# Late input projections cut into pieces of two k steps and spread over rounds 1 to 21

## The chip, the cores and the metric

The kernel runs on one core of a Trainium2 chip. The metric is the device time of one execution in microseconds (us), the smaller the better. Engines are named as in the profile: PE (TensorE, matmuls), PEld (its weight loads), DVE (VectorE), ACT (ScalarE), POOL (GpSimd), SP (SyncE, which here only issues transfers).

## The reference, cut to what matters

One layer of a decoder trunk on 1024 positions of width 1024, float32. The change lies in the first of its three parts:

```python
z = rmsnorm(h, norm_mix_g) @ w_in                 # 3840 columns: 30 blocks of 128
a_q, a_f, a_i, a_g, b_q, b_k, b_v, c_in = split(z)
o_a = hgrn2_mix(a_q, a_f, a_i, a_g, ...)          # 4 heads, a gated linear recurrence
o_b = dilated_window_mix(b_q, b_k, b_v)           # 4 heads of 64: windowed softmax attention
o_c = rwkv7_mix(c_in, ...)                        # RWKV-7
h = h + concat(o_a, o_b, o_c) @ w_out             # 8 blocks of 128 on each side
h = h + conv_glu_ffn(rmsnorm(h), ...)
h = h + sigmoid(rmsnorm(h) @ ple_gate) * (p @ ple_proj)
return rmsnorm(h)
```

## The kernel before

**Products of float32.** Every big product is made of three passes in a rounded format: `split2` and `split_x` divide an operand into a high part (a cast on ACT) and a low part (a subtraction on DVE or POOL), and `mm3` (L137, L139, L141) multiplies high by high, low by high and high by low into one PSUM bank. A weight block of 128 columns has 8 k steps; one k step on 512 positions is three matmuls, one block on one half of the positions 24.

**Stages.** First come the norm and RWKV-7, with 18 of the 22 remaining input blocks projected between its steps (`project_rest`); then HGRN and attention together, which is where the change lies (about 400 to 590 us in the profile); then the output projection (`phase_out`), the feed-forward part and the gated embedding.

**The order in HGRN and attention.** `interleave` walks a written list of letters, and each letter takes one step of a generator. A runs HGRN heads 0 and 2 one behind the other, B heads 1 and 3 from round 6 on, C attention (two groups of two heads, in the 22 rounds of `TURNS`), M what is left of `project_rest`, and F `project_late`: the last four input blocks, `self.rest` = 29, 18, 22, 23 (the values of the second attention group, the values of heads 2 and 3, the output gate of head 3). There are 36 rounds of C, A, B, F. F takes a step in rounds 1, 3, 6, 9, 12, 15, 18, 20 and 21 (`LATE`).

**What a step of F is.** One step is one half of the positions of one block: the weight load (for the first half), 24 matmuls into one PSUM tile `zp`, the `finish` (a product with the row scale, L425, or for the gate block also a sigmoid and another product, L320, L428, L430), and the store of the half to memory. After the eighth step, the ninth allocates `self.O`, the split operands of the output projection, in the memory of the split input `self.X`, and splits all finished blocks in `self.done`: 6 and 7 (RWKV), 0 and 1 (HGRN heads), 4 (attention). Each `o_split` is two casts on ACT (L160) and one subtraction each on DVE and POOL (L162). Blocks that finish later are split when they finish.

**Buffers.** `zp` comes from the PSUM pool `mx` of four banks, which HGRN and attention use for all their small results: `hsc` (scores of a level of the recurrence, L925 and L951), `hkv`, `hpo`, `vt` (transposes), `swt`, `swo`, `swd` (attention, L1130, L1143, L204). The attention scores `swq` (L1104) and the output projection `dp` have a pool of their own.

**Who orders the queues.** The framework places instructions on the engines' queues at compile time: an instruction's place in the program is its priority, a model of time says what is ready, and the queues then run in order on the chip.

Of the kernel before, what the change touches and what calls it, by code (L numbers as in the profile page):

```python
# [21 lines left out]
ND = 8  # L22
# [43 lines left out]
def interleave(order, streams):  # L66

    live = dict(streams)
    while live:
        for s in order:  # L70
            if s in live and next(live[s], STOP) is STOP:
                del live[s]


def handover(a, b, steps=14):

    for _ in range(steps):
        next(a)
        yield
    for i, _ in enumerate(b):  # L80
        if i == 1:
            for _ in a:
                yield
        yield
# [5 lines left out]
class Trunk:  # L90
# [231 lines left out]
    def phase_mix(self):  # L322
        nc, tc = self.nc, self.tc
        self.mix_norm()
        with tc.tile_pool(name="slots", bufs=1) as slots:
            self.slots, self.NSLOT = slots, 8
            self.rwkv()
        self.O, self.done = None, []
        for p in (0, 1):
            self.o_split(6 + p)  # L330
        with tc.tile_pool(name="hg", bufs=1) as slots, tc.tile_pool(name="sw", bufs=1) as sp:
            self.slots, self.NSLOT = slots, 11
            self.hgrn_setup()
            self.sp = sp
            self.swmask = sp.tile([P, T], F32, name="swmask")
            nc.scalar.dma_start(self.swmask, self.a["swm"])
            A = handover(self.hgrn_head(0), self.hgrn_head(2))
            B = handover(self.hgrn_head(1), self.hgrn_head(3))
            order = ["C", "A"] + ["M"] * 24
            for r in range(36):  # L340
                order += "C" * (r in self.TURNS) + "A" + "B" * (r > 5) + "F" * (r in self.LATE)
            interleave(order, {"A": A, "B": B, "C": self.swa(sp), "F": self.project_late(self.rest), "M": self.more})

    LATE = (1, 3, 6, 9, 12, 15, 18, 20, 21)

    TURNS = [i * 33 // 22 for i in range(1, 23)]

# [84 lines left out]
    def project_late(self, js):  # L432


        nc = self.nc
        for j in js:
            w = self.load_w(self.a["w_in"][j])
            t = self.keep.tile([P, T], F32, tag="zst", name=self.nm("zst"), bufs=2)
            d = self.zpool.tile([P, T], F32, tag=f"z{j}", name=f"z{j}")
            kind = (j - 8) % 4 if j < 24 else 2  # L440
            turn = j < 24 and kind < 3
            for hf in (0, 1):
                ps = self.mxp.tile([P, HT], F32, tag="mx", name=self.nm("zp"))
                self.dense({hf: ps}, w, self.X, ND, halves=(hf,))
                dst = slice((hf ^ turn) * HT, ((hf ^ turn) + 1) * HT)
                r = self.R[:, hf * HT:(hf + 1) * HT]
                self.finish(kind, t[:, dst], *((ps[:, ::-1], r[:, ::-1]) if turn and hf else (ps, r)))
                nc.sync.dma_start(d[:, dst], t[:, dst])
                if hf:
                    self.z[j] = d  # L450
                yield
        self.O = self.xall()
        for k in self.done:
            self.o_split(k)

    def zload(self, j, pool_slot, eng=None):
        t = pool_slot("zl")
        (eng or self.nc.sync).dma_start(t, self.z[j])
        return t
# [1315 lines left out]
```

## Time and profile before

| | |
|---|---|
| runs, us | 1438.21, 1439.37, 1434.61 (median 1438.21) |
| the profiled execution, us | 1434.87, of which the span of its instructions is 1433.1 |
| mean granted clock of TensorE | 0.992 |
| busy share of the span | PE 97%, PEld 78%, DVE 74%, ACT 42%, POOL 27% |
| matmuls of `zp` | 192, from 402.2 to 521.2 us of the span |
| last late store | 526.6 us |

A busy PE is not a PE at its peak: matmuls overlap, and a stretch counts as busy though its clock is half of the full one.

### The profile page before, as it was taken

To read this page: it belongs to the slowest core of one execution; us is meant where nothing else is said; L and a number is where in the kernel's file an instruction comes from. 1 tells how busy PE (TensorE), PEld (TensorE's weight loads), DVE (VectorE), ACT (ScalarE), POOL (GpSimd) and SP (SyncE) were. 2 spreads that over 40 slices of the span, in tenths; PEclk is the share of its full clock that TensorE was granted. 3 is DMA by queue.
4 is the path that set the end of the run, shared out by engine and by line. 5 is a ranking of instruction groups with operands and counts; after the bars stand their busy time and mean duration, and the time that the engine had idled before them with its cause. 6 is when DMAs were issued, how large, how long until landed. Compare 5 with 4: busy or idle time off the path is not lost.

```text
span 1433.1 us, 22327 instructions
## 1 busy us (share of the span) xinstructions
PE 1383.1 (97%) x8638; PEld 1119.6 (78%) x8638; DVE 1054.6 (74%) x1635; ACT 604.1 (42%) x1015; POOL 380.9 (27%) x281
## 2 busy tenths in 40 slices
PE   6999999999999989999999999999999999999996
PEld 5778777777777867787788888888888888888885
DVE  6487353864657767458888888988898799777675
ACT  6511323123145465244544444334344444455542
POOL 2321012201122231121245445445453000002332
PEclk9999999999999989999999999999999999999998
DMA  6124112240442211652323232333324973441343
GB/s 219 45 81 118 61 35 80 71 119 31 150 145 104 85 50 46 234 200 100 143 79 105 96 110 98 109 110 110 102 98 136 340 244 105 123 147 45 133 156 116
DMA packets 79674, 167.61 MB, mean 117 GB/s; under 512 B 19920, under 2 KB 22224, under 8 KB 79568
## 3 DMA queue, kind: packets, MB, share of 16 engines
q1 hardware_dynamic: 66176, 146.39, 30.4%
q10 hardware_dynamic: 12368, 15.99, 3.3%
q0 software_dynamic: 1024, 3.80, 0.7%
q8 instruction: 68, 1.11, 0.3%
q14 instruction: 38, 0.31, 0.1%
HBM read 119.76 MB, written 46.40 MB: 116 GB/s over the span
## 4 chain that ended last, share of the span: by engine, by line
PE 50%; issue 2%; DVE 1%; POOL 1%; ACT 0%; DMA 0%; POOLq 0%; ACTq 0%; DVEq 0%
PE bg L1262 16%; PE bv L1262 12%; PE bv L1556 7%; PE bg L1556 7%; PE bv L137 1%; PE bv L139 1%; PE bv L141 1%; PE bg L137 1%; PE bg L141 1%; PE bg L139 1%; PE dp L141 1%; PE dp L139 1%; PE dp L137 1%; POOL wlo L116 0%; DVE h L1288 0%
## 5 line engine op out<-in xcount | busy, mean ns | idle before, releaser
L137 PE MATMUL dp<-xh,whi 128*128 128x512 f32 x544 | 189.1, 406 | 9.8 <-ACT xh L380 9.6
L139 PE MATMUL dp<-xl,whi 128*128 128x512 f32 x544 | 183.6, 395 | 0.7 <-DVE xl L381 0.6
L141 PE MATMUL dp<-xh,wlo 128*128 128x512 f32 x544 | 181.9, 393 | 0.3 <-POOL wlo L116 0.3
L116 POOL TENSOR_TENSOR wlo<-wraw,whi 128x512 fp32r<-128x512 f32 x60 | 81.1, 1353 | 309.0 <-ACT whi L114 278.9
L116 POOL TENSOR_TENSOR wlo<-raw,whi 128x512 fp32r<-128x512 f32 x84 | 134.7, 1622 | 76.1 <-ACT whi L114 76.1
L114 ACT CAST whi<-wraw 128x512 fp32r<-128x512 f32 x120 | 73.0, 617 | 179.9 <-PE dp L139 140.6
L1262 PE MATMUL bg<-t,whi 128*128 128x512 f32 x352 | 133.2, 389 | 0.0
L137 PEld LDWEIGHTS dp<-xh,whi 128*128 128x128 f32 x544 | 99.7, 189 | 34.3 <-ACT xh L380 9.6
L139 PEld LDWEIGHTS dp<-xl,whi 128*128 128x128 f32 x544 | 102.0, 188 | 25.1 <-DVE xl L381 2.4
L141 PEld LDWEIGHTS dp<-xh,wlo 128*128 128x128 f32 x544 | 102.4, 189 | 23.1 <-POOL wlo L116 0.8
L116 POOL TENSOR_TENSOR wlo<-s,whi 128x512 fp32r<-128x512 f32 x44 | 64.2, 1459 | 173.2 <-ACT whi L114 173.2
L1556 PE MATMUL bg<-t,whi 128*128 128x512 f32 x308 | 95.2, 390 | 0.0
L1556 PE MATMUL bv<-t,whi 128*128 128x512 f32 x308 | 94.8, 389 | 0.0
L114 ACT CAST whi<-raw 128x512 fp32r<-128x512 f32 x88 | 52.6, 619 | 94.6 <-issue 48.6
L114 ACT CAST whi<-s 128x512 fp32r<-128x512 f32 x66 | 38.9, 620 | 121.1 <-PE bg L1262 113.3
L1262 PEld LDWEIGHTS bg<-t,whi 128*128 128x128 f32 x352 | 66.1, 188 | 13.7
L190 POOL TENSOR_TENSOR rst<-rst,mhalf 128x4 f32<-128x4 f32 (+1 forms) x9 | 10.9, 1214 | 242.7 <-DVE rst L186 225.5
L116 DVE TENSOR_TENSOR wlo<-wraw,whi 128x512 fp32r<-128x512 f32 x60 | 46.6, 777 | 34.5 <-ACT whi L114 27.6
L1556 PEld LDWEIGHTS bv<-t,whi 128*128 128x128 f32 x308 | 57.8, 188 | 12.0
L1262 PE MATMUL bg<-t,wlo 128*128 128x512 f32 x176 | 67.2, 389 | 0.0
L1556 PEld LDWEIGHTS bg<-t,whi 128*128 128x128 f32 x308 | 57.8, 188 | 11.9
L1552 ACT CAST t<-t 128x512 fp32r<-128x512 f32 x77 | 47.8, 622 | 40.5 <-PE bv L1556 27.8
(415 smaller groups left out, 3396.1 us busy)
## 6 DMA issues: line engine op xcount, KB each, us to landing
raw<-in_ffn_up_dram SPq DMA_DIRECT2D x44, 512.0 KB, 3.5
wraw<-in_w_in_dram SPq DMA_DIRECT2D x30, 512.0 KB, 3.5
z<-zst SPq DMA_DIRECT2D x18, 512.0 KB, 3.4
gb<-ct SPq DMA_DIRECT2D x33, 256.0 KB, 2.1
t<-gb SPq DMA_DIRECT2D x33, 256.0 KB, 2.7
t<-gt SPq DMA_DIRECT2D x33, 256.0 KB, 2.7
zl<-z SPq DMA_DIRECT2D x16, 512.0 KB, 4.2
wraw<-in_ple_gate_dram SPq DMA_DIRECT2D x16, 512.0 KB, 3.4
```

The costliest lines, as they stand in the source:

```text
L114: self.cast = nc.scalar.copy(hi, src).ins
L116: eng.tensor_tensor(lo, src, hi.bitcast(F32), ALU.subtract)
L137: nc.tensor.matmul(ps[hf], wh, xh[hf], start=first, stop=False)
L139: nc.tensor.matmul(ps[hf], wh, xl[hf], start=False, stop=False)
L141: nc.tensor.matmul(ps[hf], wl, xh[hf], start=False, stop=last)
L190: nc.gpsimd.tensor_tensor(r2, r, self.mhalf[:, :n], ALU.pow)
L1262: nc.tensor.matmul(ps, w[part == 2][:, s], X[k][part == 1], start=start and k == part == 0, stop=k == 3 and part == 2, skip_group_check=no ...
L1552: nc.scalar.copy(xh, x)
L1556: nc.tensor.matmul(ps[m], wt[part == 2][:, m * P:(m + 1) * P], (xh, xl)[part == 1], start=k == part == 0, stop=k == NK - 1 and part == 2)
```

## The change

A step of F becomes two k steps (6 matmuls) of one half; every fourth step also finishes and stores the half, so that there are 32 steps in place of 8. A function `late(r)` in place of the list spreads them over rounds 1 to 21: ten rounds take one step and eleven take two. With two, one stands ahead of B and one behind it. `self.O` is allocated in round 22 in place of round 21, and the five splits are taken one a round, in rounds 22 to 26.

```diff
             for r in range(36):
-                order += "C" * (r in self.TURNS) + "A" + "B" * (r > 5) + "F" * (r in self.LATE)
+                n = self.late(r + 1) - self.late(r)
+                order += "C" * (r in self.TURNS) + "A" + "F" * (n // 2) + "B" * (r > 5) + "F" * (n - n // 2)
...
-    LATE = (1, 3, 6, 9, 12, 15, 18, 20, 21)
+    def late(self, r):
+        return min(32, max(0, r - 1) * 32 // 21) + max(0, min(6, r - 22))
...
                 ps = self.mxp.tile([P, HT], F32, tag="mx", name=self.nm("zp"))
-                self.dense({hf: ps}, w, self.X, ND, halves=(hf,))
+                for k in range(ND):
+                    self.mm3({hf: ps}, w(k), self.X[k], k == 0, k == ND - 1, (hf,))
+                    if k in (1, 3, 5):
+                        yield
...
         self.O = self.xall()
         for k in self.done:
             self.o_split(k)
+            yield
```

## The prediction

> **What bounds the kernel now.** I read the busy time of the engines by stretches first, because the page's 97% for PE says nothing of one stage. PE, PEld, DVE, ACT and POOL follow each stretch with the count of their instructions, then the granted clock, the share of the transfer engines and GB/s.
>
> ```profile
> 400.00:420.00 20.00, 19.93 (x174) 14.61 (x174) 11.38 (x28) 10.78 (x27) 7.87 (x7) 1.00 0.38 120
> 460.00:480.00 20.00, 20.00 (x266) 17.35 (x265) 16.16 (x32) 8.00 (x18) 5.46 (x6) 1.00 0.32 118
> 480.00:500.00 20.00, 20.00 (x175) 17.03 (x174) 14.60 (x38) 12.72 (x30) 4.76 (x4) 1.00 0.25 80
> 500.00:520.00 20.00, 17.05 (x83) 11.42 (x83) 13.27 (x24) 9.94 (x17) 4.04 (x3) 0.74 0.20 71
> 520.00:540.00 20.00, 18.24 (x195) 13.91 (x194) 15.34 (x34) 17.85 (x36) 9.36 (x9) 1.00 0.14 49
> 540.00:560.00 20.00, 18.48 (x197) 14.91 (x196) 15.94 (x34) 11.82 (x21) 4.16 (x3) 1.00 0.15 54
> 580.00:600.00 20.00, 18.15 (x83) 14.32 (x82) 8.78 (x12) 1.67 (x4) 2.92 (x2) 1.00 0.64 249
> ```
>
> Up to 500 us PE has no hole: whatever the order of the late projections is there, PE is the bound and reordering can't gain. From 500 to 520 PE is idle for 3 us and its clock is 0.74. That is a half clock for (1 - 0.74) x 20 / 0.5 = 10.4 us. From 520 on there are small holes. So I took the timeline of PE, then of DVE and ACT, around 500 us (start, length, engine, line, operation, count, and in brackets the idle time ahead and what ended it).
>
> ```profile
> 502.99 0.39 PE L141 MATMUL zp<-xh,wlo 128*128 128x512 f32 x1
> 505.94 1.34 PE L1104 MATMUL swq<-zl,zl 64*128 64x512 f32 x4
> 510.23 1.12 PE L951 MATMUL hsc<-qt,ks 128*64 128x64 f32 x16 [2.95 <-DVE qt L964]
> 512.01 2.50 PE L1104 MATMUL swq<-zl,zl 64*128 64x512 f32 x4
> 514.44 0.79 PE L139 MATMUL zp<-xl,whi 128*128 128x512 f32 x1
> 518.87 0.47 PE L141 MATMUL zp<-xh,wlo 128*128 128x512 f32 x1
> 519.18 0.39 PE L137 MATMUL zp<-xh,whi 128*128 128x512 f32 x1
> 519.41 0.39 PE L139 MATMUL zp<-xl,whi 128*128 128x512 f32 x1
> ...
> 499.45 0.69 DVE L162 TENSOR_TENSOR xl<-zl,xh 128x512 fp32r<-128x512 f32 x1 [2.25 <-ACT xh L160]
> 503.59 1.23 DVE L1033 TENSOR_TENSOR ho<-ho,hrs 128x1024 f32<-128x1024 f32 x1 [1.75 <-POOL hrs L1031]
> 509.40 0.68 DVE L964 TENSOR_TENSOR qt<-qt,hT 128x512 f32<-128x512 f32 x1
> 519.76 0.69 DVE L116 TENSOR_TENSOR wlo<-wraw,whi 128x512 fp32r<-128x512 f32 x1 [4.58 <-ACT whi L114]
> ...
> 501.37 0.62 ACT L160 CAST xh<-ob 128x512 fp32r<-128x512 f32 x1 [0.99 <-PE zp L141]
> 515.69 0.62 ACT L160 CAST xh<-zl 128x512 fp32r<-128x512 f32 x1 [3.64 <-PE zp L141]
> 519.11 0.62 ACT L114 CAST whi<-wraw 128x512 fp32r<-128x512 f32 x1 [2.80 <-PE zp L139]
> ```
>
> The reader sees a seesaw. While PE does the 24 matmuls of round 18 (497.7 to 503), DVE runs dry; its work then comes in one burst from 503.59 to 515 without a gap, the next level of the recurrence gets its `qt` only at 509.40, and PE stands for 2.95 us. The clock falls to half. In round 20 the same again: DVE stands for 4.58 us behind the lump, and ACT, whose queue is in order, stands for 3.64 and 2.80 us, since the split casts wait until the lump has left `self.X`. The bill of that comes behind 520.
>
> ```profile
> 524.08 0.69 PE L1104 MATMUL swq<-zl,zl 64*128 64x512 f32 x1 [0.60 <-DVE sden L1114]
> 531.62 1.15 PE L925 MATMUL hsc<-zl,hk 128*64 128x64 f32 x32 [1.16 <-ACT ob L1144]
> 559.47 1.06 PE L1039 MATMUL vt<-cst,ho 128*128 128x128 f32 x8 [1.18 <-DVE ho L1033]
> 584.73 1.06 PE L1039 MATMUL vt<-cst,ho 128*128 128x128 f32 x8 [1.79 <-DVE ho L1033]
> ```
>
> The last two follow a chain inside one head (square, sum, power on POOL, scaling, transpose), which the change does not touch.
>
> **What the change can give back.** Same matmuls, same casts, same transfers; only places change. (1) The hole of 2.95 us. (2) The half clock while PE works. Between 514.44 and 518.87 eleven matmuls start; at the full rate, 0.23 from 519.18 to 519.41, their ten intervals and one would take 2.3 us in place of 4.4, so 2.1 lost. From 510.23 to 514.44 lie 16 small matmuls, one of `zp` and four of `swq`, 4.2 us; half of that, 2.1, is lost if all of it is clock-bound. Together 4.2. (3) The holes of 0.60 and 1.16, which follow the clogged ACT queue. Sum 2.95 + 4.2 + 1.76 = 8.9 us. I take all of it, for with six matmuls at a time (6 x 0.23 = 1.4 us) neither DVE nor ACT is starved for longer than a level's own latency. The lower end is nothing (a hole of this kind opens elsewhere, see the rivals), the upper 8.9 plus the holes of 1.18 and 1.79, 11.9.
>
> **What it costs: more changes of work on PE.** Up to 24 more stretches of `zp`. The ends of the first lump show the price:
>
> ```profile
> 402.23 0.50 PE L137 MATMUL zp<-xh,whi 128*128 128x512 f32 x1
> 402.56 0.39 PE L139 MATMUL zp<-xl,whi 128*128 128x512 f32 x1
> 402.80 0.40 PE L141 MATMUL zp<-xh,wlo 128*128 128x512 f32 x1
> 407.59 0.39 PE L141 MATMUL zp<-xh,wlo 128*128 128x512 f32 x1
> 407.91 0.88 PE L951 MATMUL hsc<-qt,ks 128*64 128x64 f32 x16
> ```
>
> The first matmul holds the next back by 0.33 in place of 0.23, the last by 0.32: 0.2 us for each stretch, taking the change into it as no dearer than the one between two small kinds that it replaces. 24 x 0.2 = 4.8 at most; nothing at least, where the queue puts pieces side by side. Of 24 I take 18: rounds with two pieces (eleven of them) have only a level of B in between, and some will meet. 18 x 0.2 = 3.6 us, all on the path, as PE has no hole before 500.
>
> **What it costs: PSUM.** A `zp` bank is now held for four pieces. The pieces are 32 in 21 rounds, so four take 2.6 rounds; rounds 1 to 20 last some 6 us each (the first row below: 402.2 to 521.2), so a bank is held for 16 us, one behind the other, and the small results have three banks in place of four. They are held briefly:
>
> ```profile
> L137 PE MATMUL zp<-xh,whi x64: 387/389/796, 402.2 to 521.2; 128*128 128x512 f32 x64
> 526.31 0.69 PE L951 MATMUL hsc<-qt,ks 128*64 128x64 f32 x16
> 527.04 0.45 DVE L953 COPY_PREDICATED hS<-cmask,hsc 128x256 f32<-128x256 uint8 x1 [0.49 <-PE hsc L951]
> PE hsc L925 <- ACT ob L1144: 1.2, 1, 1.2
> ```
>
> A typical score tile is free again 1.2 us after its first matmul. The last row (from the waits of PE alone, 400 to 532 us) is its one wait of over 1 us for a bank: the scores need nothing that ACT's copy of `swo` makes but its bank. So with three banks I take one more such wait, 1.2 us; the lower bound is zero, the upper one such wait in every second of the 21 rounds, 12 us.
>
> **What moves and costs nothing.** Each half's finish, one store and, per block, one load on SP, two casts and the POOL and DVE subtractions move with it; counts are unchanged. The weight tiles turn over in the same order, but their release is spread, so ACT's waits of the 2.80 kind shrink; if they don't, they cost what they cost now. The results come in time: piece 8 falls in round 6 and attention reads block 29 in round 12; pieces 16 and 24 fall in rounds 11 and 16, read in rounds 22 and 29; block 23 ends in round 21 and is read in round 33. SP passes nothing that waits on them: only loads of `w_out` and of head inputs stand behind a store, and these have rounds to spare. The five splits, 10 casts of 0.62 on ACT with 5 subtractions each on DVE and POOL, now rank behind rounds 22 to 26. That takes them from ahead of attention's copies; the first reader is the output projection, whose first matmul starts near 552, so a round or two of delay has cover. If the projection came first, it would wait at most one split, 0.62 + 1.28 us (a cast and POOL's subtraction).
>
> **Sum.** -8.9 + 3.6 + 1.2 = -4.1 us against the profiled execution's 1434.87: 1430.8, so 1431. From about 590 us on PE is the bound almost to the end, so what is won early arrives. The profiled execution is a quick one: the runs were 1434.61 to 1439.37 with median 1438.21. What made two of them 3 to 5 us longer no trace shows; a second half-clock stretch would be of that size (4.2), and then the change could take that too. I add nothing for it. About 0.3%, 4.3 us, is what a measurement here can tell from no change.
>
> [...] The half clock began behind a hole of 2.95 us and, by the 0.74, lasted 10.4 us. [...]
>
> **Rivals.**
> - *The hole only moves.* DVE is 14 to 16 of 20 us busy in this stretch, and some burst may still meet a PE without filler. For it: rounds 18 to 21 used to bring 48 late matmuls and now bring 42, in small pieces that run out. Against: one piece is then always near. Then 7.2 us return: 1430.8 + 7.2 = 1438, within the bound.
> - *Three PSUM banks don't do* (slower). PE queues in order, so one small result without a bank holds everything behind it, and neighbours such as transposes (`vt`, four a head) and two to four `swt` a round want several banks at once. Each such wait is 1.16 us by the row at 531.62. It decides from nine on: -8.9 + 3.6 + 9 x 1.16 = +5.1. With twelve, 1443.5. Against: 1.2 us of holding. [...]
> - *Pieces meet and later holes close too.* No price for switches, and some of 1.18 and 1.79: 1434.9 - 8.9 - 1.5 = 1424.5.
> - *Nothing happens,* because the planner puts the pieces back together into lumps: 1434.9.
>
> **Chances.** Forecast 0.50 (its own range 1426 to 1435, by the switches at 0 to 4.8 and the bank waits at 0 to 4); the hole moves 0.17; PSUM 0.16; meet and close 0.12; nothing 0.05. The range reaches from just below the fourth case to between the hole's and the PSUM case: 1423 to 1441. Measured against a median that may stand above the profiled time, some two thirds of the forecast is faster by over 0.3%, with the fourth case 0.46; the rest of it, most of the moved hole and nothing give 0.34 the same; PSUM and a bad moved hole 0.20 slower.
>
> **What would show it.** Right: in PE's timeline pieces of 6 of `zp` from about 402 to 515; no half clock near 510; ACT's waits on `zp` under 1 us; casts of the splits spread behind 515; `dp` starting some 4 to 9 us earlier than 552. Wrong: PE holes before 500 that ACT or DVE copies of another tile end (banks), or the clock at half in another stretch, or stretches of 24 `zp` as before.

## The result, and the profile after

The changed kernel took 1442.73 us (median; 1438.74 to 1446.60), the kernel before 1438.28 (1434.61 to 1442.54): ratio 1.003, 95% interval 1.0021 to 1.0039. It is slower by some 4.4 us where 1431 was forecast. The profiled execution has a span of 1439.2 us.

The stretches of the stage in the changed kernel, with the columns of those shown of before:

```profile
400.00:420.00 20.00, 20.00 (x176) 14.55 (x174) 12.59 (x30) 10.97 (x27) 8.05 (x7) 1.00 0.42 144
460.00:480.00 20.00, 17.61 (x153) 13.38 (x152) 13.98 (x25) 7.65 (x14) 6.60 (x6) 0.91 0.39 139
500.00:520.00 20.00, 18.72 (x146) 13.20 (x144) 14.34 (x34) 12.17 (x30) 4.72 (x3) 1.00 0.33 108
520.00:540.00 20.00, 15.61 (x175) 11.73 (x175) 19.94 (x29) 15.84 (x30) 11.99 (x9) 1.00 0.16 56
540.00:560.00 20.00, 17.61 (x165) 12.83 (x165) 15.81 (x39) 12.45 (x25) 2.26 (x2) 1.00 0.22 74
```

The hole and the long half clock near 510 are gone (PE's clock is 1.00 there). But PE is idle for 4.4 us from 520 to 540, where DVE is busy for all of the 20 us with 29 instructions; before it had 34 in 15.3. DVE is not given more to do: its instructions are longer. The waits of PE from 400 to 590 us of the changed kernel (engine, line and tile waiting, what ended it, total us, times, longest):

```profile
PE hsc L957 <- DVE pT L1137: 2.4, 1, 2.4
PE hsc L931 <- DVE zst L432: 2.2, 1, 2.2
PE vt L1045 <- DVE hS L959: 1.7, 1, 1.7
PE vt L1045 <- DVE ho L1039: 1.6, 1, 1.6
PE swt L1136 <- ACT ob L1150: 1.4, 1, 1.4
PE swt L1136 <- DVE hS L959: 1.2, 1, 1.2
PE swt L1136 <- DVE pT L1137: 0.7, 1, 0.7
```

Only the fourth is a wait for data. A transpose `swt` needs nothing from `hS`, nor a score `hsc` anything from `zst` or from attention's `pT`: they wait for the PSUM bank that this copy or product reads out last. These six sum to 9.6 us; before there was one such wait of over 1 us, of 1.2.

Why DVE reads out late is seen in the timeline, DVE first, POOL below, PE last:

```profile
521.99 2.31 DVE L911 TENSOR_TENSOR qt<-zl,zl 128x1024 f32<-128x1024 f32 x1
526.47 0.67 DVE L432 TENSOR_TENSOR zst<-zst,zp 128x512 f32<-128x512 f32 x1
527.06 0.69 DVE L320 TENSOR_TENSOR zp<-zp,rstd 128x512 f32<-128x512 f32 x1
527.66 2.12 DVE L962 COPY_PREDICATED hS<-cmask,hS 64x256 f32<-64x256 uint8 x2
529.68 1.51 DVE L963 COPY_PREDICATED hS<-cmask,hS 64x256 f32<-64x256 uint8 x1
531.97 0.68 DVE L432 TENSOR_TENSOR zst<-zst,zp 128x512 f32<-128x512 f32 x1
...
521.90 1.31 POOL L162 TENSOR_TENSOR xl<-ob,xh 128x512 fp32r<-128x512 f32 x1 [0.46 <-ACT xh L160]
526.78 2.69 POOL L162 TENSOR_TENSOR xl<-oc,xh 128x512 fp32r<-128x512 f32 x2 [0.40 <-ACT xh L160]
529.44 1.45 POOL L162 TENSOR_TENSOR xl<-zl,xh 128x512 fp32r<-128x512 f32 x1
...
532.71 1.15 PE L931 MATMUL hsc<-zl,hk 128*64 128x64 f32 x32 [2.25 <-DVE zst L432]
```

The two copies of L962 (L956 in the kernel before) took 0.93 together before, and here 2.12; the one of L963 (L957) took 0.44 and takes 1.51, to 531.19, just behind the end of POOL's subtraction at 530.89. The products with an operand from PSUM (L320, L432) run at 0.7 us through the same time. Over the stage of the changed kernel 26 DVE instructions without an operand in PSUM lay beside a TENSOR_TENSOR of POOL for more than 0.3 us, and 18 of them took at least 0.2 us longer than is usual for their kind; of 19 such neighbours with an operand in PSUM none did, nor did any DVE instruction without such a neighbour. So here an instruction of DVE that works on SBUF alone often (18 of 26) stands while such an instruction of POOL runs. Six rows of before show those two lines of DVE, and where the same subtractions of POOL lay then:

```profile
529.30 0.93 DVE L956 COPY_PREDICATED hS<-cmask,hS 64x256 f32<-64x256 uint8 x2
530.12 0.44 DVE L957 COPY_PREDICATED hS<-cmask,hS 64x256 f32<-64x256 uint8 x1
...
516.39 1.28 POOL L162 TENSOR_TENSOR xl<-zl,xh 128x512 fp32r<-128x512 f32 x1 [3.07 <-ACT xh L160]
520.77 1.29 POOL L162 TENSOR_TENSOR xl<-ob,xh 128x512 fp32r<-128x512 f32 x1 [3.10 <-ACT xh L160]
522.96 1.27 POOL L162 TENSOR_TENSOR xl<-oc,xh 128x512 fp32r<-128x512 f32 x1 [0.90 <-ACT xh L160]
525.41 1.28 POOL L162 TENSOR_TENSOR xl<-oc,xh 128x512 fp32r<-128x512 f32 x1
```

The first two subtractions lie whole in the pauses of DVE that the lump of round 20 made: 4.58 us ahead of 519.76 and another of 1.67 us ahead of 522.12. The seesaw that I read as loss was also POOL's free time.

Why DVE stands there, no run shows.

### The profile page after: what moved, and what is told of

Same layout as the page of the kernel before. It is cut to its first block, busy times and chain, and to the rows that moved or that the text cites. A ratio compares the mean times of both kernels' runs of the same rounds, so it can differ in the third digit from the quotient of the medians.

```text
span 1439.2 us, 22329 instructions
## 1 busy us (share of the span) xinstructions
PE 1383.8 (96%) x8638; PEld 1115.3 (77%) x8638; DVE 1062.1 (74%) x1635; ACT 600.9 (42%) x1013; POOL 383.2 (27%) x281
## 4 chain that ended last, share of the span: by engine, by line
PE 49%; issue 2%; DVE 1%; POOL 1%; ACT 0%; DMA 0%; POOLq 0%; ACTq 0%; DVEq 0%
PE bg L1268 16%; PE bv L1268 12%; PE bv L1562 7%; PE bg L1562 7%; PE bv L137 1%; PE bv L139 1%; PE bv L141 1%; PE bg L137 1%; PE bg L141 1%; PE bg L139 1%; PE dp L141 1%; PE dp L139 1%; PE dp L137 1%; POOL wlo L116 0%; DVE h L1294 0%
## 5 line engine op out<-in xcount | busy, mean ns | idle before, releaser
L139 PE MATMUL dp<-xl,whi 128*128 128x512 f32 x544 | 183.8, 396 | 0.1
L1268 PEld LDWEIGHTS bg<-t,whi 128*128 128x128 f32 x352 | 66.0, 188 | 13.7
L116 DVE TENSOR_TENSOR wlo<-wraw,whi 128x512 fp32r<-128x512 f32 x60 | 48.0, 800 | 30.8 <-ACT whi L114 23.9
L1562 PEld LDWEIGHTS bg<-t,whi 128*128 128x128 f32 x308 | 57.7, 188 | 11.9
```

The source lines that it names most:

```text
L116: eng.tensor_tensor(lo, src, hi.bitcast(F32), ALU.subtract)
L139: nc.tensor.matmul(ps[hf], wh, xl[hf], start=False, stop=False)
L1268: nc.tensor.matmul(ps, w[part == 2][:, s], X[k][part == 1], start=start and k == part == 0, stop=k == 3 and part == 2, skip_group_check=no ...
L1562: nc.tensor.matmul(ps[m], wt[part == 2][:, m * P:(m + 1) * P], (xh, xl)[part == 1], start=k == part == 0, stop=k == NK - 1 and part == 2)
```

## The experiments

Theory PORT (a name only; no run shows a port): POOL's subtractions, no longer beside a standing DVE, hold it up, and banks come free late. Theory BANK: the late pieces hold one of four banks without a pause, and that alone makes the small results wait. The table was worked out from each trace in the same way. "Stage" is the time from the first score matmul to the transposes of the last head. "Holes" are all idle times of PE in it. "Half clock" is the time in it at which half the clock was granted. "DVE over" is what DVE's instructions took above the typical one of their kind and shape. Stages can be compared closer than spans: the program ahead is not edited, yet in these profiles the stage began anywhere from 400.3 to 407.4 us. The four columns on the right are still of one execution each, and the half clock partly changes from one to the next (last section). The ratio is to executions of the kernel before that were taken beside each kernel's own, so it can differ a little from the quotient of the medians.

| kernel | median, us | ratio to before (95%) | stage | holes | half clock | DVE over |
|---|---|---|---|---|---|---|
| before | 1438.28 | | 183.6 | 8.7 | 10.2 | 5.0 |
| changed | 1442.73 | 1.0030 (1.0021 to 1.0039) | 188.4 | 14.7 | 3.4 | 11.8 |
| dve_splits | 1436.22 | 0.9985 (0.9972 to 0.9999) | 183.2 | 8.5 | 3.4 | 6.0 |
| lumps_hold | 1443.69 | 1.0036 (1.0023 to 1.0048) | 186.9 | 13.0 | 6.8 | 11.6 |
| splits_only | 1439.21 | 1.0005 (0.9987 to 1.0022) | 181.9 | 8.2 | 10.2 | 5.3 |
| pieces_only | 1444.84 | 1.0042 (1.0025 to 1.0059) | 187.1 | 12.3 | 6.8 | 10.2 |
| before_dve | 1441.45 | 1.0018 (1.0007 to 1.0028) | 188.9 | 10.4 | 17.1 | 7.4 |
| hold_dve | 1440.15 | 1.0010 (1.0001 to 1.0018) | 185.9 | 11.9 | 3.4 | 7.7 |
| packed | 1438.38 | 1.0003 (0.9994 to 1.0011) | 184.4 | 11.0 | 6.8 | 9.7 |
| k1_dve | 1434.00 | 0.9973 (0.9962 to 0.9983) | 182.6 | 7.9 | 3.4 | 3.5 |
| pool_dummy | 1444.52 | 1.0037 (1.0022 to 1.0052) | 189.2 | 12.2 | 10.2 | 11.5 |
| packed_dve | 1434.15 | 0.9968 (0.9954 to 0.9983) | 182.3 | 8.3 | 3.4 | 5.9 |
| k1_pool | 1437.71 | 1.0003 (0.9989 to 1.0017) | 184.4 | 9.5 | 10.2 | 7.4 |
| k1_packed_dve | 1435.22 | 0.9978 (0.9965 to 0.9992) | 182.3 | 8.3 | 3.4 | 5.9 |
| before_held | 1449.63 | 1.0076 (1.0060 to 1.0091) | 194.6 | 12.1 | 23.9 | 8.1 |
| dve_held | 1446.90 | 1.0060 (1.0045 to 1.0075) | 193.4 | 11.6 | 17.1 | 6.7 |

**The two halves of the change, each alone.** First the splits one a round, with the lumps kept:

```diff
-    LATE = (1, 3, 6, 9, 12, 15, 18, 20, 21)
+    LATE = (1, 3, 6, 9, 12, 15, 18, 20, 22, 23, 24, 25, 26, 27)
...
             self.o_split(k)
+            yield
```

> The kernel before with one edit: the memory of the split input passes to the output's operands in round 22 and the five splits come one a round in rounds 22 to 26; the late projections stay lumps of 24 in the old rounds. PORT: the POOL subtractions come when DVE is busy, 1439 to 1443, with DVE's time above typical at 8 us or more. BANK: no loss, 1434 to 1439.

Then the pieces, with all five splits in one step in round 21:

```diff
-                order += "C" * (r in self.TURNS) + "A" + "F" * (n // 2) + "B" * (r > 5) + "F" * (n - n // 2)
+                order += "C" * (r in self.TURNS) + "A" + "F" * (n // 2) + "B" * (r > 5) + "F" * (n - n // 2) + "F" * (r == 21)
...
-        return min(32, max(0, r - 1) * 32 // 21) + max(0, min(6, r - 22))
+        return min(32, max(0, r - 1) * 32 // 21)
...
             self.o_split(k)
-            yield
```

> The changed kernel with the splits put back: all five in one step in round 21, behind the last piece. BANK: as the changed kernel, 1441 to 1445. PORT: if it is the late rank of the splits that makes them collide, back to 1437 to 1440; if the pieces alone let DVE and POOL meet, as the changed kernel.

The splits' new rank shows no loss (1.0005, 0.9987 to 1.0022); the pieces alone cost the whole loss (1.0042). That PORT expected a loss of `splits_only` was wrong: with lumps DVE has its pauses, whatever the rank (DVE over 5.3).

**POOL's half of the splits to DVE.**

```diff
-            self.split_x(self.O[k], hf, self.o[k][:, hf * HT:(hf + 1) * HT], alt=hf)
+            self.split_x(self.O[k], hf, self.o[k][:, hf * HT:(hf + 1) * HT])
```

> The changed kernel with one edit: both subtractions of each split run on DVE, none on POOL (10 POOL instructions of 1.3 us less, up to 10 DVE instructions of 0.68 us more over the stage). Theory PORT (POOL's split subtractions now run while DVE works, and hold DVE's instructions up; DVE then frees PSUM banks late): DVE's time above its typical lengths falls from 11.8 us to about 6, PE's holes between the first score and the last head's transposes fall from 14.7 us to 10 or less, time 1436 to 1440 against 1438.3 before. Theory BANK (pieces hold one of four PSUM banks without a pause, small results wait for a bank): holes stay at 13 us or more, and DVE has more to do: 1442 to 1446.

It gives 6.5 us, and the interval of its ratio to the kernel before ends just below 1. The stretch of 20 us, DVE now at 38 instructions in 18.85 us where the changed kernel had 29 in 19.94, and PE's longest waits for a bank:

```profile
520.00:540.00 20.00, 18.27 (x176) 12.71 (x173) 18.85 (x38) 15.96 (x31) 4.52 (x4) 1.00 0.23 79
...
PE hsc L957 <- DVE pT L1137: 2.4, 1, 2.4
PE hsc L957 <- ACT hV L986: 0.7, 1, 0.7
PE vt L1045 <- DVE hS L959: 0.5, 1, 0.5
PE swt L1136 <- ACT ob L1150: 0.3, 1, 0.3
```

The same edit in the kernel before:

> The kernel before with both subtractions of each split on DVE, nothing else. PORT: of DVE's 5.0 us above typical lengths in the stage only some 2 belong to the splits' POOL work, as it fell while DVE stood still; so a gain of 0 to 3 us, 1436 to 1439, and clearly less than the 6.5 that the same edit gave in the changed kernel. If the edit is worth 4 to 7 us here too, it has nothing to do with the change.

There it costs 2.6 us (1.0018), where 0 to 3 were to be gained: DVE takes the work on top of its bursts, and a second hole came, with the half clock at 17.1 us. POOL's help pays with lumps and hurts with pieces.

**POOL's work without its result.** To `dve_splits` one subtraction per split is added on POOL, whose result nobody reads:

```diff
+        scr = self.sp.tile([P, HT], mybir.dt.bfloat16, tag="scr", name=self.nm("scr"), bufs=1)
+        self.nc.gpsimd.tensor_tensor(scr, self.o[k][:, HT:], self.O[k][0][1].bitcast(F32), ALU.subtract)
```

> The changed kernel with the splits wholly on DVE (1436.2), and with one subtraction per split added on POOL that reads the same two operands and writes a scratch tile that nobody reads (8 POOL instructions of some 1.3 us, no result needed). PORT: POOL's reading alone holds DVE up; DVE's time above typical goes from 6.0 us to 9 or more, PE's holes from 8.5 to 11 or more, 1439 to 1445. If POOL's part was slow as a step on the way to the output projection and not as a neighbour of DVE: no change, 1434 to 1438.

The loss is back: 8.3 us above `dve_splits` by the medians, 7.5 by the two ratios. The copy of L963 stands again, and now that of L964 (0.44 in the changed kernel), beside the dummies:

```profile
528.31 1.52 DVE L963 COPY_PREDICATED hS<-cmask,hS 64x256 f32<-64x256 uint8 x1
529.86 1.36 DVE L964 COPY_PREDICATED hS<-cmask,hS 64x256 f32<-64x256 uint8 x1
...
526.82 2.70 POOL L1174 TENSOR_TENSOR scr<-oc,xh 128x512 bf16<-128x512 f32 x2 [4.25 <-ACT xh L160]
529.60 1.33 POOL L1174 TENSOR_TENSOR scr<-zl,xh 128x512 bf16<-128x512 f32 x1
```

No other step depends on the dummies' result. They can also delay what stands behind them in POOL's own queue; that is seen, but small: beside `dve_splits` ACT waits 1.8 us more for POOL from 505 to 592 us (2.1 against 0.3), DVE 1.7 us less (2.2 against 3.9), and PE never waits for it. So PORT is shown as a cause. In this kernel the late copies hold up attention's read of the scores, and PE then stands 2.71 us ahead of `swq` for a bank of the scores' own pool.

**The bank held without pieces.** In the kernel before, the first k step of each late half is issued right behind the half ahead of it (`begin` allocates `zp` and issues k = 0):

```diff
+        ps = begin(0)
+        for i, (j, hf) in enumerate(units):
...
+            for k in range(1, ND):
+                self.mm3({hf: ps}, cur["w"](k), self.X[k], False, k == ND - 1, (hf,))
...
+            if i + 1 < len(units):
+                ps = begin(i + 1)
```

> The kernel before with one edit: the first k step (3 matmuls) of each late half is given right behind the half before it, so that a late half holds a PSUM bank at all times from round 1 to round 20, while the other 21 matmuls stay one lump and the splits stay in round 21. BANK: waits of PE for a bank appear as in the changed kernel, holes 12 us or more, 1441 to 1445. PORT: nothing of weight changes, 1436 to 1440.

> The lumps whose bank is held at all times (4.5 us slower than before), now with both subtractions on DVE. PORT: the loss there also comes from POOL holding DVE up while banks are scarce: back to 1437 to 1440. BANK alone: the scarce bank costs by itself, 1441 to 1445.

The loss is there without pieces (1.0036), so the hold matters, and that PORT expected nothing of weight was wrong. But DVE over rose too, to 11.6, and with the splits on DVE most of the loss goes by the runs (1.0010): 1440.15 lies between what the two theories expected. By the two traces less goes: the stage is 1.0 us shorter, its holes 11.9 against 13.0. That left open what a bank costs by itself. The first two kernels made for this did not hold the bank. A matmul of one column wrote a spare tile in round 1, and a copy of one column was to release it behind round 20:

```diff
+        held = self.mxp.tile([P, HT], F32, tag="mx", name=self.nm("held"))
+        nc.tensor.matmul(held[:, 0:1], self.ident, self.ones, start=True, stop=True)
...
+        let = self.spool.tile([P, 1], F32, tag="let", name=self.nm("let"), bufs=1)
+        nc.vector.tensor_copy(let, held[:, 0:1])
```

> The kernel before with one PSUM bank of the four taken out of use from round 1 to round 21 (a matmul of one column writes it, a copy of one column reads it at the end; no other step is moved). Small results have three banks, two while a lump runs. BANK: the loss of the changed kernel or more, 1441 to 1448. PORT as the cause and banks only as the place where it shows: 1437 to 1441.

> The changed kernel with the splits on DVE (1436.2) and one more PSUM bank out of use from round 1 to round 21, so that the small results have two. BANK: 4 us or more longer, 1440 to 1450. If a bank less costs little as long as POOL leaves DVE alone: 1436 to 1439.

They took 1450.88 (1.0092, 1.0076 to 1.0108) and 1449.04 (1.0078, 1.0065 to 1.0091), as BANK expects, and for another reason: the copy ran at 407.9 us, and the stages are as long as without it (183.8 and 182.0 us). The 12 us lie behind the stage (last section). `dve_splits` was run once more beside them:

> The changed kernel with splits on DVE again, one look beside the next.

It gave 1439.03 in a single run, stage 183.1. Then the release was made to depend on the last late half, with no tile added to SBUF:

```diff
-        let = self.spool.tile([P, 1], F32, tag="let", name=self.nm("let"), bufs=1)
-        nc.vector.tensor_copy(let, held[:, 0:1])
+        nc.tensor.matmul(held[:, 0:1], t[:, HT:HT + P], self.ones, start=True, stop=True)
```

> The kernel before with one PSUM bank of the four out of use from round 1 to the end of the last late half: two matmuls of one column write it, the second one reads the last late half's result and so can't come early; no tile of SBUF is added. Small results have three banks, two while a lump runs. BANK: the loss of the changed kernel or more inside the stage, 1441 to 1448. If banks cost little while POOL and DVE keep out of each other's way: 1437 to 1441.

> The changed kernel with the splits on DVE (1436.2) and one more bank out of use in the same way, so that the small results have two until the last late half. BANK: 4 us or more longer, 1440 to 1450. If a bank less costs little as long as POOL leaves DVE alone: 1436 to 1439.

The bank was held to 540.7 and 543.3 us, and the stages grew by 11.0 and 10.2 us, with POOL's half of the splits and without. So to take a bank away costs by itself, and needs no collision. But it does not do so as BANK has it. These are the longest waits of PE, first in `before_held`, then in `dve_held`:

```profile
PE swq L1107 <- DVE sden L1117: 4.8, 2, 2.6
PE vt L1042 <- DVE ho L1036: 2.9, 2, 1.8
PE hsc L954 <- DVE qt L967: 1.6, 2, 1.1
...
PE swq L1113 <- DVE sden L1123: 3.3, 1, 3.3
PE vt L1048 <- DVE ho L1042: 2.9, 2, 1.7
PE swt L1139 <- ACT ob L1153: 2.5, 2, 1.7
```

Only the last is a wait for a bank of `mx`. The first and the fourth are for a bank of the scores' own pool, which L1117 and L1123 read out, and the others are for data. Read as above, the waits for banks of `mx` sum to 1.9 us in `before_held` against 1.5 in before, and to 4.9 in `dve_held` against 4.2 in `dve_splits`. The stages grew by holes and clock: 3.4 and 3.1 us more of holes, and 13.7 us more of half clock in each, which costs at most half of that, 6.9 (an estimate: in the profile of before, matmuls of `zp` start every 0.43 us at half clock, from 515.03 to 515.46, and every 0.23 at the full one); together some 10 of the 11.0 and 10.2. Why the scores are read out later is not shown. It may be the order that the planner makes with a bank less: in `dve_held` PE's queue has 43 stretches of `zp` in place of 31.

So in the changed kernel waits for banks are seen (the six above), and that the loss needs POOL's work is shown by `dve_splits`. How much a held bank adds there by itself is not.

**A shorter hold, finer pieces.** Pieces two a round, for two rounds in a row:

```diff
-                n = self.late(r + 1) - self.late(r)
+                n = 2 * (r in self.LATE) + 2 * (r - 1 in self.LATE) + (22 <= r < 28)
...
+    LATE = (1, 3, 6, 9, 12, 15, 18, 20)
```

> The changed kernel with the four pieces of a half given in two rounds in a row, two in each, starting in the old rounds 1, 3, 6, 9, 12, 15, 18, 20; splits one a round as in the changed kernel, POOL still does its half of them. A bank is held for about one round and a half in place of 2.6, with gaps between halves. BANK: at least half of the loss returns, 1437 to 1441. PORT: POOL and DVE still meet, 1441 to 1445.

> Pieces of two k steps, two a round for two rounds (1438.4), and the splits on DVE. BANK and PORT as two conditions of one loss: with the bank held for a shorter time DVE's lateness costs less, so the edit brings less than the 6.5 us that it brought at the long hold: 1435 to 1438.

The first brings back the whole loss (1.0003) though POOL still does its half, which PORT did not expect. Its holes fall from 14.7 to 11.0 us; but its waits of over 1 us for a bank still sum to 6.7, against 8.9 in the changed kernel, so that the shorter hold is what wins is argued and not shown. The second is 0.9968, the quickest beside `k1_dve`; the edit brings 4.2 us here, less than 6.5 as expected, though 1434.15 lies below the range. Pieces of one k step (`if k < ND - 1`, 64 in place of 32), with the splits on DVE, on POOL, and packed:

> The changed kernel with the splits on DVE (1436.2) and pieces of one k step: 64 pieces of 3 matmuls in rounds 1 to 21. The bank is held as long; there are some 30 more stretches of late matmuls on PE. At the predicted 0.2 us for a stretch 6 us more, 1441 to 1444; at the 0.07 us that the accounts of the two traces leave, 2 us more, 1437 to 1440.

> 64 pieces of one k step (1434.0 with the splits on DVE), now with POOL doing its half of the splits as in the changed kernel. PORT: the loss returns, 1438 to 1443, DVE's time above typical at 8 us or more against 3.5. If the size of the pieces is what counts: 1433 to 1436.

> Pieces of one k step, four a round for two rounds in a row from the old rounds on, splits on DVE. If shorter hold and finer pieces add up: 1431 to 1434. If DVE and ACT set the pace by now: as 64 pieces spread evenly, 1433 to 1437.

`k1_dve` came out below both of its ranges. The price of a stretch was not tested by these: the planner put the pieces side by side, and PE's queue had 35 stretches of `zp` where 31 were. With POOL's half the 64 pieces are at 1.0003, without it at 0.9973: PORT again, at 3.7 us, though DVE over is 7.4 and not the 8 expected. Packing adds nothing to pieces of one step.

## Why the prediction was wrong

- **The seesaw, right as a reading and wrong as a balance.** The hole of 2.95 us near 507 and its half clock went, and so did DVE's pauses behind the lump; for the holes of 0.60 and 1.16 others of 0.5 and 1.4 came, ended by the same engines. What the clock gave is in the runs: at the same mean granted clock of 0.991 the changed kernel took 1441.93 to 1443.95 us against 1436.05 to 1436.81 before, some 7 us, of which 2 to 3 came back by a better clock (median 0.991 against 0.989). But I booked the pauses as pure loss. They were where POOL's subtractions ran without a neighbour. One small reading was off as well: the half clock began at 508.8, inside the hole (507.28 to 510.23) and not behind it.
- **"What moves and costs nothing" failed.** For the splits I priced the delay of their reader and not their neighbours: POOL's 1.3 us instructions now lie beside a DVE without pauses, and DVE over rose by 6.8 us. Without them the kernel is 6.5 us quicker (`dve_splits`), and with dummies in their place 7.5 to 8.3 us slower again (`pool_dummy`): this term, put at nothing, is larger than the whole loss of 4.4.
- **The PSUM term was mis-sized:** 1.2 us taken, 12 as the upper end. Measured in the changed kernel: six waits, 9.6 us, against 1.2 in before. I took one more wait of the one size that I had seen, since a score tile is usually free again after 1.2 us. But what counts is the hold when DVE is late: the scores written at 521.03 in the changed kernel were read out at 524.64, after 3.6 us. The rival of three banks put its point of decision at nine waits of 1.16; six waits of 1.6 on average, with a half clock behind one, were enough, together with DVE's lateness that made them long, to pass the 0.3%.
- **The hole does move as well.** One of 2.39 us opened at 467, with 3.4 us of half clock behind it, which is a sign of being wrong that the prediction had named. It ends on a bank, and it is also in `dve_splits` and `packed`, so it does not hang on POOL's half of the splits.
- **Switches: 3.6 taken, about 2.5 left over.** `dve_splits` has 31 stretches of `zp` against 9, and the same holes. Halving the time that PE worked at half clock (8.8 and 3.4 us), it saved 2.7 us there; yet the stage is only 0.4 shorter. So some 2.5 us are left, 0.1 for each of 22 stretches: an estimate from two traces, which no run tested.
- **What is left of the sum** without POOL's split subtractions: `dve_splits`, 1436.2, is 2.2 below before by its ratio of 0.9985 (3.0 by the medians of its own round, 1439.18 and 1436.22). That is about half of the 4.1 that I summed.

## What to carry to other kernels

Before evening out a seesaw between two engines, ask which third engine lives in its pauses: here POOL's half of the splits was worth having only while DVE had pauses (giving it to DVE cost 2.6 us with lumps and brought 6.5 with pieces). A piece of work cut up to fill gaps holds its accumulator from its first part to its last; here giving the parts close together won the loss back (`packed`, 1.0003). Price a PSUM bank by how late its readers can be, not by how long they usually take (3.6 us in the changed kernel, 1.2 in the one before). When moving work on POOL, list the instructions of DVE beside its new place that have no operand in PSUM: of 26 such in the changed kernel 18 took at least 0.2 us longer than usual, of 19 with one none.

## What the runs showed of the hardware

A hole of 2.39 us on PE came with 3.4 us at half clock right behind it (changed kernel, near 470), and one of 2.95 with 10.2 us (before, near 510). The size of the hole does not decide it alone. In `dve_bank2` the same hole of 2.39 us near 470 brought no half clock. A hole of 2.38 us near 363 us, ahead of every edit, stands in all nineteen profiles; nine of them have a window of 3.4 us at half clock at its end, and ten, before and changed among them, have none. In the profiles all half clock within the stage came in whole multiples of 3.41 us: one stretch from 469.70 to 473.11 in the changed kernel, one from 508.80 to 519.04 before, and 3.4, 6.8, 10.2, 17.1 and 23.9 in the table.

Such windows come and go in the stages ahead too: none in the profile of before, one near 94 us in the changed kernel's, three in that of `pool_dummy`, four in that of `pieces_only`. The scatter of the runs goes with the clock: of the executions of the kernel before that were taken beside the experiments, those with a mean granted clock of 0.986 took 1442.11 to 1443.80 us, those with 0.992 took 1433.95 to 1435.51. This bears on what the prediction left open, why two of its three runs were longer.

A tile of one column (4 bytes a partition) in the pool of small tiles came with slower matmuls in later stages. The groups of the same 308 matmuls of the last big product, in the kernel before and in `before_bank` (busy us, mean ns):

```profile
L1556 PE MATMUL bv<-t,whi 128*128 128x512 f32 x308 | 94.8, 389 | 0.0
```

```profile
L1560 PE MATMUL bv<-t,whi 128*128 128x512 f32 x308 | 96.6, 395 | 0.0
```

Both kernels with this tile are longer behind the stage, by 12.5 and 10.5 us against the kernels that they were made from (860.8 and 859.8 against 847.0 to 850.6 us in all others), and `before_held`, which holds a bank without it, is not (849.1). What makes them longer is not shown.
